# Last output projection: the first pair's parts requested ahead of the first products, in tiles of their own, and the sum weights' slabs requested one step ahead

## The chip, the cores and the metric

The kernel runs on one core of one Trainium2 chip. The metric is the device time of one execution in microseconds (us). Three runs of the kernel before gave 999.89, 1000.36 and 1002.28; the median is 1000.36 us. One more execution was taken with the hardware profiler; all views below come from that one. In them PE is TensorE's matmul, PEld its weight load, DVE is VectorE, ACT is ScalarE, POOL is GpSimd, SP is SyncE, which mostly issues DMAs; a name with a q behind it (SPq) is that engine's instruction queue.

## The reference

Two decoder layers over 1024 tokens of width 1024. What matters here is the end of each layer: three head groups give 1024 gated columns (attention 512, retention 256, gated linear attention 256), these are projected, normalised and added to the residual.

```python
a_out = sliding_window_attention(aq, ak, av, sinks) * jax.nn.silu(ag)
...
r_out = rms_norm(r).reshape(B, S, RET_W) * jax.nn.silu(rg)
...
g_out = rms_norm(g, gla_norm_gain).reshape(B, S, GLA_W) * jax.nn.silu(gg)

y = jnp.concatenate([a_out, r_out, g_out], axis=-1) @ w_out
return x + gate * rms_norm(y, post_gain)
```

All arrays are float32, and the outputs have to keep that accuracy.

## The kernel before, in words

**Numbers.** A float32 matrix is kept as two rounded halves (a high half and the rest, the low half), and a product is three passes: high by high, low by high, high by low (`PASSES`). A product of a 128-token tile's 512 input columns with a 512 x 512 block of weights is 12 matmuls of 128 x 512. Splitting is a rounding copy (high half) and a subtraction (low half); which engine does it is set in the table `EN`: "A" for ScalarE, "V" for VectorE, "G" for GpSimd.

**The last layer's projection** (`last_output`, from L1326) goes over eight token tiles t. The first two (`PLAIN = 2`) are computed one by one, the other six as three pairs. A pair of tiles (e, o), split into two column halves, and the weights, split into 2 x 2 blocks, form a 2 x 2 block product, which is done with seven block products instead of eight (Strassen's scheme in Winograd's form). It needs sums of the inputs (`Pair`) and sums of the weights (T1 to T4; W00, W10, W11 are plain blocks). The plain tiles use W00, W10, W11 and T1 too, with four products each: W00 for both tiles, then for each tile T1 and W11 into one bank and W10 into another.

**The pair's steps.** `Pair.parts` (L1280) requests four 256 KB parts from DRAM (`mixF`), one for each tile and column half. `Pair.sum` requests the plain halves of tile e (`ma<-mixS`, four DMAs) and makes four sums on VectorE (keys ms0 to ms3, L1296 to L1299). `early` splits two sums into an `mx` tile (for T2 and T1), `late` the other two (for W11 and T3). `a22` requests tile o's second half (`a<-mixS`, two DMAs) for T4. In the loop over pairs the products come in the order W00, W10, T2, T1, W11, T3, T4. After W00, `kept` (L1332) copies the bank to SBUF on ScalarE, which lets the bank go.

**The weights' sums.** `sw_second` (L593) is a job: in each of four steps k it requests four slabs of 256 KB of `w_last`, makes differences and a sum on VectorE (L569, L571, L599), and splits the three results into the arena (`sw_split`: high halves on ScalarE, L149; low halves of T2 on VectorE, of T3 and T4 on GpSimd, L564).

**Buffers.** Tags share rotating buffers: `t2` has 10 (parts, the gates' temporaries, the outputs `yg` and the residual tiles of `finish` all draw on them), `st` has 5 (weight slabs, the squares' discarded results, `a22`), `mx` has 2. PSUM banks: `mm` has 3, `aux` 5.

**The order.** TensorE runs in the order in which the program is written out. A planner keeps a clock `clk` of TensorE's estimated time and a list of jobs (generators); `pump` steps each job when its due time has come. The due times are the latencies in table `L`; `sw1` is the distance of the steps of `sw_second`. The instructions of the other engines are ordered by the framework, from the program's order and its own estimate of when operands and buffers are ready; then each engine runs its queue strictly in that order, so an instruction that waits holds up all that stand behind it. This holds for SyncE, which issues nearly all loads (`dma` with key "lw", "lmix", "lx" and so on).

**Around it.** Before the projection, the last attention jobs write their output to DRAM (`aoS<-t`), read it back transposed (`t<-aoS`), multiply it with the gate (L1581), and write it to `mixF` (unsplit) and, split (L151, L1593), to `mixS`. The pair loop's first pair is tiles 2 and 3, from the first half of the tokens; the gates that come last are of tiles 4 to 7. `finish` (L1239) reads the residual (`t<-xs`), adds, and writes the output from ScalarE's queue.

Of the kernel before, what the change touches and what calls it, by code (L numbers as in the profile page):

```python
# [10 lines left out]
F32 = mybir.dt.float32  # L11
# [6 lines left out]
P = 128  # L18
# [31 lines left out]
PLAIN = 2  # L50
# [43 lines left out]
def trunk(ctx: ExitStack, tc: tile.TileContext, ins, cst, out):  # L94
    nc = tc.nc
# [7 lines left out]
    gp = ctx.enter_context(tc.tile_pool(name="work", bufs=2))  # L103
# [9 lines left out]
    def t2(dt=F32):  # L113
        return gp.tile([P, 512], dt, tag="t2", name=nm("t2"), bufs=B2)
# [4 lines left out]
    def stage():  # L119
        return gp.tile([P, 512], F32, tag="st", name=nm("st"), bufs=BST)  # L120
# [4 lines left out]
    def mm():  # L125
        return ps.tile([P, 512], F32, tag="mm", name=nm("mm"), bufs=MMB)
# [17 lines left out]
    def eng(k):  # L144
        return G if EN[k] == "G" else V
# [37 lines left out]
    def lat(key, l):  # L183

        return L[key + "@1"] if l and key + "@1" in L else L[key]

# [257 lines left out]
    def tables_T():  # L444

        for p in range(NP_):
            yield L["tt1"]
            rep_ = t2()
# [143 lines left out]

    def sw_second():  # L593
        drain()
        for k in range(4):
            s3, x = sw_load(k, 0, 1), sw_load(k, 1, 1)
            sw_diff(s3, 1, k, x, s3)
            s2, s4 = sw_load(k, 0, 0), sw_load(k, 1, 0)
            eng("sd").tensor_tensor(s2, s3, s2, ALU.add)  # L599
# [675 lines left out]
    class Pair:  # L1275
# [10 lines left out]
        def sum(self):  # L1286
            e = self.e
            self.a = []
            for c in range(2):
                s = gp.tile([P, NT * P], F32R, tag=f"kT{c}", name=nm("ma"), bufs=1).rearrange(  # L1290
                    "p (a k q) -> p a k q", a=2, k=4)
                for a in range(2):
                    dma("lmix", f(s[:, a]), mixS[e, :, a, 4 * c:4 * c + 4])
                self.a.append(s)
            a21, a22, a11, a12 = self.p
            eng("ms0").tensor_tensor(a22, a21, a22, ALU.add)  # L1296
            eng("ms1").tensor_tensor(a21, a11, a21, ALU.subtract)
            eng("ms2").tensor_tensor(a11, a22, a11, ALU.subtract)
            eng("ms3").tensor_tensor(a12, a12, a11, ALU.subtract)  # L1299
            self.sums = a22, a11, a21, a12  # L1300
# [25 lines left out]
    def last_output(l, load_mix):  # L1326
        gcol = [modg[l][:, 0:512], modg[l][:, 512:1024]]

        def kept(src=None):
            s = gp.tile([P, 4, 129], F32, tag="smx", name=nm("kept"), bufs=SMB).rearrange("p h q -> p (h q)")[:, 0:512]  # L1330
            if src is not None:
                A.activation(s, src, AF.Copy)  # L1332
            return s
# [14 lines left out]
        nxt = None  # L1348
        if PLAIN:
            m = {0: load_mix(l, 0)}  # L1350
        for p in range(PLAIN // 2):
            x, ss, yg = [], [], []
            for t in (2 * p, 2 * p + 1):
                if t + 1 < PLAIN:
                    m[t + 1] = load_mix(l, t + 1)
                x.append(mm())
                ss.append(small(2))
                yg.append([t2(), t2()])
                prod(x[-1], slots(m[t])[0], "W00")
                if t == 0:  # L1360
                    job(sw_second())
                    pump()
            s1 = [kept(x[0]), kept(x[1])]
            for i, t in enumerate((2 * p, 2 * p + 1)):
                a = slots(m[t])
                z = aux()
                prod(z, a[0], "T1", True, False)
                prod(z, a[1], "W11", False, True)
                summed(yg[i][1], z, s1[i], ss[i][:, 1:2], 1)
                y = mm()  # L1370
                prod(y, a[1], "W10")
                summed(yg[i][0], y, s1[i], ss[i][:, 0:1], 0)
                job(finish(l, t, ss[i], yg[i]))
                if t == PLAIN - 2:
                    nxt = Pair(l, p + 1)
                    nxt.parts()
                    nxt.sum()
                pump()
                if t == PLAIN - 2:
                    nxt.early()  # L1380
                if t == PLAIN - 1:
                    nxt.late()
        for p in range(PLAIN // 2, NP_):
            cur, nxt = nxt, Pair(l, p + 1) if p + 1 < NP_ else None
            e, o = 2 * p, 2 * p + 1
# [282 lines left out]
L = {"sw1": 0.4, "ld1": 1.2, "ld2": 1.2, "ld1@1": 1.2, "ld2@1": 1.27, "swW00": 0.0, "swT1": 0.0, "swW11": 0.4, "swW10": 0.5, "tt1": 8.0, "tt2": 1.75, "tb1": 24.5, "tb2": 0.75, "pf3": 13.2, "pf1": 6.35, "pf2": 4.16, "mod1": 4.6, "mod2": 4.0, "mod3": 13.29, "mod4": 7.04, "mod5": 3.36, "mod6": 9.04, "pre1": 7.44, "kv1": 3.1, "kv2": 2.11, "aq1": 6.0, "aq7": 6.0, "ag1": 5.44, "aq2": 2.4, "aq6": 5.2, "aq3": 10.21, "aq4": 7.36, "aq5": 3.6, "hn1": 8.93, "hn2": 2.85, "gz1": 11.18, "gz2": 8.13, "gl1": 2.76, "gd3": 15.9, "gc1": 0.62, "gc2": 1.94, "gc3": 1.33, "gc4": 0.87, "gc6": 0.86, "gc5": 1.14, "rc1": 0.8, "rc2": 1.09, "rc3": 5.87, "rc4": 2.51, "fin1": 7.28, "lay1": 1.13, "gc4@1": 0.93, "mod2@1": 4.0, "mod3@1": 15.1, "mod5@1": 3.36, "mod6@1": 4.11, "pre1@1": 7.44, "kv1@1": 2.79, "kv2@1": 5.28, "aq1@1": 4.8, "aq7@1": 5.28, "ag1@1": 6.25, "aq2@1": 0.82, "aq6@1": 6.0, "aq3@1": 10.9, "aq4@1": 4.4, "aq5@1": 5.15, "hn1@1": 8.12, "hn2@1": 2.85, "gz1@1": 15.91, "gz2@1": 10.94, "gl1@1": 4.6, "gd3@1": 15.9, "gc1@1": 0.48, "gc2@1": 1.94, "gc3@1": 1.33, "gc6@1": 0.86, "gc5@1": 1.04, "rc1@1": 0.37, "rc2@1": 0.84, "rc3@1": 1.9, "rc4@1": 2.79, "fin1@1": 4.28, "lay1@1": 1.7}  # L1668
CHUNK = 7
LAG = 2  # L1670
VDB = 8
# [41 lines left out]
```

## Time and profile before

| what | value |
|---|---|
| median of three runs | 1000.36 us |
| the profiled execution's own time | 1005.29 us |
| its span, first to last instruction | 1003.6 us |
| mean granted TensorE clock | 0.989 |
| DMA moved, mean rate | 148.73 MB, 148 GB/s |

Stretches of the end of the span, by what TensorE does in them (times from the span's start; busy us of each engine, share of the DMA engines):

| stretch, us | TensorE's work | PE | DVE | ACT | DMA share |
|---|---|---|---|---|---|
| 897.0 to 906.7 | last gate projections, attention | 9.70 | 6.10 | 4.03 | 0.77 |
| 906.7 to 919.2 | W00 of tiles 0 and 1, T1 and W11 of tile 0 | 12.50 | 8.26 | 4.67 | 0.87 |
| 919.2 to 930.5 | W10 of tile 0, tile 1 | 11.30 | 7.56 | 4.81 | 0.76 |
| 944.5 to 953.0 | T1, W11, T3 of the first pair | 8.50 | 5.46 | 1.40 | 0.96 |
| 962.2 to 973.4 | second pair | 11.20 | 9.37 | 3.33 | 0.88 |
| 996.0 to 1003.6 | tail: norm, residual, store | 0.03 | 4.23 | 0.51 | 0.37 |

A view of TensorE's timeline has one line for a run of equal instructions: start, duration, engine, line of the kernel, operation, output and inputs by the program's names, shape, count, and in brackets the idle time before it with the instruction that ended it. All products have the same line, L165, a helper's.

### The profile page before, as it was taken

The page shows a single profiled execution, that of the slowest core. Times are in us where ns is not written, and L with a number is a line of the kernel's source. Part 1 is how long each engine was busy: PE and PEld are TensorE (multiplying, and loading weights), DVE is VectorE, ACT ScalarE, POOL GpSimd, SP SyncE. Part 2 cuts the span into 40 slices and gives each one's busy share as a digit, 9 for nine tenths or more (in the row PEclk, how much of TensorE's full clock was granted, in tenths as well). Part 3 has the DMA queues.
Part 4 walks back from the last instruction along what each step waited for, and adds up shares of the span by engine and source line. Part 5 has one row for each costly group of instructions (what it writes and reads, how often), then busy time and mean ns, then how long its engine had stood idle before and what let it go on. Part 6 is the DMA issues. An engine that isn't in the chain of part 4 may idle for free.

```text
span 1003.6 us, 19610 instructions
## 1 busy us (share of the span) xinstructions
PE 972.6 (97%) x7137; PEld 827.5 (82%) x7137; DVE 683.7 (68%) x1680; ACT 409.0 (41%) x1152; POOL 234.7 (23%) x275
## 2 busy tenths in 40 slices
PE   5899999999999999999999999999999999999896
PEld 1599999888998777778889999998999777777675
DVE  3788857678666778654677385775766577566786
ACT  2486312233332656632555332133333267563231
POOL 2310001223320234420122010122332034444000
PEclk8899999999999999999999999999999999999998
DMA  8842513623235355597555241352222435477883
GB/s 306 297 145 79 166 43 102 189 78 121 65 94 172 90 156 168 167 283 234 178 171 166 82 139 32 117 171 68 64 82 88 122 91 153 129 227 237 252 272 132
DMA packets 112172, 148.73 MB, mean 148 GB/s; under 512 B 11998, under 2 KB 63688, under 8 KB 112076
## 3 DMA queue, kind: packets, MB, share of 16 engines
q1 hardware_dynamic: 106380, 137.92, 44.2%
q10 hardware_dynamic: 5696, 9.56, 2.6%
q8 instruction: 56, 0.92, 0.4%
q14 instruction: 40, 0.33, 0.1%
HBM read 109.17 MB, written 36.18 MB: 145 GB/s over the span
## 4 chain that ended last, share of the span: by engine, by line
PE 80%; DMA 8%; DVE 7%; issue 2%; POOL 1%; ACT 1%; SPq 1%; ACTq 0%; POOLq 0%; DVEq 0%
PE mm L165 62%; PE aux L165 14%; PE aux L180 5%; DMA st<-in_w_in_dram 2%; DMA st<-in_w_last_dram 1%; POOL sm L635 1%; DMA xk<-in_x_dram 1%; DMA a<-mixS 1%; DMA t<-aoS 1%; DMA t<-mixF 1%; DVE arena L533 1%; DVE t L328 0%; SPq L154 0%; DMA t<-in_x_dram 0%; DMA t<-xs 0%
## 5 line engine op out<-in xcount | busy, mean ns | idle before, releaser
L165 PE MATMUL mm<-arena 128*128 128x256 f32 (+2 forms) x1824 | 300.0, 318 | 1.8 <-ACT arena L704 1.8
L165 PE MATMUL mm<-arena,arena 128*128 128x256 f32 (+2 forms) x1824 | 299.0, 317 | 0.0
L165 PEld LDWEIGHTS mm<-arena 128*128 128x128 f32 x1824 | 255.3, 191 | 26.6 <-issue 4.1
L165 PEld LDWEIGHTS mm<-arena,arena 128*128 128x128 f32 x1824 | 252.9, 188 | 25.2 <-issue 4.4
L635 POOL TENSOR_TENSOR sm<-sm,mhalf 128x1 f32<-128x1 f32 (+1 forms) x64 | 55.8, 871 | 347.0 <-DVE sm L634 328.4
L165 PE MATMUL mm<-arena,mx 128*128 128x512 f32 (+1 forms) x564 | 132.6, 392 | 3.7 <-ACT kept L1332 3.7
L165 PEld LDWEIGHTS mm<-arena,mx 128*128 128x128 f32 x564 | 103.0, 190 | 28.2 <-ACT kept L1332 4.2
L149 ACT ACTIVATE t<-aux 128x256 f32<-128x256 f32 (+2 forms) x124 | 55.7, 467 | 74.9 <-PE aux L180 63.8
L149 ACT ACTIVATE arena<-st 128x512 fp32r<-128x512 f32 x94 | 55.9, 626 | 54.8 <-DMA st<-in_w_in_dram 19.7
L533 POOL TENSOR_TENSOR arena<-st,arena 128x512 fp32r<-128x512 f32 x31 | 43.3, 1399 | 134.1 <-ACT arena L149 96.8
L923 POOL TENSOR_TENSOR smx<-smx,sm 128x512 f32<-128x512 f32 x32 | 36.5, 1142 | 127.6 <-DVE sm L922 118.4
L533 DVE TENSOR_TENSOR arena<-st,arena 128x512 fp32r<-128x512 f32 x77 | 59.5, 794 | 4.5 <-ACT arena L149 2.4
L919 ACT ACTIVATE smx<-smx,sm 128x129 f32<-128x129 f32 x128 | 49.9, 392 | 28.8 <-DVE sm L916 28.8
L180 PE MATMUL aux<-c_ident,t 128*128 128x128 f32 (+1 forms) x292 | 48.8, 284 | 5.8 <-DVE t L666 5.5
L364 DVE SCALAR_TENSOR_TENSOR acc<-st,c_act,acc 128x512 f32<-128x512 f32 x60 | 45.5, 759 | 12.6 <-DMA st<-in_w_mod_dram 12.0
L180 PEld LDWEIGHTS aux<-c_ident,t 128*128 128x128 f32 (+1 forms) x292 | 35.4, 145 | 13.5 <-DVE t L666 7.4
L698 ACT ACTIVATE t<-aux,mod,mod 128x128 f32<-128x128 f32 x68 | 26.0, 460 | 44.5 <-DVE t L1239 18.3
L165 PEld LDWEIGHTS aux<-t,mx 32*128 32x128 f32 (+1 forms) x896 | 39.5, 187 | 3.9 <-issue 1.9
L967 ACT ACTIVATE t<-aux 128x256 f32<-128x256 f32 x32 | 12.3, 384 | 73.3 <-PE aux L165 60.7
L165 PE MATMUL aux<-t,mx 32*128 32x32 f32 (+1 forms) x896 | 40.6, 272 | 0.0
L914 DVE COPY_PREDICATED smx<-c_curmask,aux 128x256 f32<-128x256 int32 x64 | 25.5, 447 | 18.9 <-ACT smx L149 15.8
L1239 DVE SCALAR_TENSOR_TENSOR t<-t,sm,t 128x512 f32<-128x512 f32 x32 | 23.9, 779 | 17.9 <-DMA t<-in_x_dram 12.3
(220 smaller groups left out, 1378.2 us busy)
## 6 DMA issues: line engine op xcount, KB each, us to landing
st<-in_w_in_dram SPq DMA_DIRECT2D x96, 256.0 KB, 3.7
st<-in_w_mod_dram SPq DMA_DIRECT2D x64, 256.0 KB, 3.0
mx<-mixS SPq DMA_DIRECT2D x20, 512.0 KB, 5.8
mixS<-t SPq DMA_DIRECT2D x72, 128.0 KB, 2.6
st<-in_w_last_dram SPq DMA_DIRECT2D x36, 256.0 KB, 3.7
wm<-in_w_mod_dram SPq DMA_DIRECT2D x12, 512.0 KB, 7.2
t<-in_x_dram SPq DMA_DIRECT2D x24, 256.0 KB, 4.3
t<-tabS SPq DMA_DIRECT2D x16, 256.0 KB, 3.7
```

The costliest lines, as they stand in the source:

```text
L149: A.activation(dst, src, AF.Copy)
L165: T.matmul(dst, lhsT, rhs, start=start, stop=stop)
L180: T.transpose(dst, src, idn)
L364: V.scalar_tensor_tensor(acc, wt, c_act[:, k:k + 1], acc, ALU.mult, ALU.add)
L533: e.tensor_tensor(lo, st, f(hi), ALU.subtract)
L635: G.tensor_tensor(r, r, mhalf[:, :w], ALU.pow)
L698: A.activation(hf[:, ks], at[kt], AF.Identity, scale=gain, bias=shift)
L914: V.copy_predicated(sv, curmask.unsqueeze(1).to_broadcast((P, 2, P)), pv[:, :, n // P - 1, :])
L919: A.activation(sm[:, h, :], sm[:, h, :], AF.Exp, bias=mx[:, h:h + 1], accum_out=sums[:, h:h + 1])
L923: eng("pn").tensor_tensor(sm[:, :, 0:128], sm[:, :, 0:128], rs.unsqueeze(2).to_broadcast((P, 4, P)), ALU.mult)
L967: A.activation(sq, po, AF.Square)
L1239: V.scalar_tensor_tensor(xt[j], yg[j], r, xt[j], ALU.mult, ALU.add)
```

## The change

It touches the last projection and two constants.

- The parts of a pair get a tag of their own, `mp`, with four buffers, instead of `t2`.
- `Pair.sum` is cut in two: `upper` requests the four `ma` tiles, `sum` makes the sums.
- For the first pair, `parts` and `upper` are called after W00 of both plain tiles, before T1 of tile 0; before, they came after W10 of tile 0. `sum` comes after tile 1's T1 and W11, `early` after its W10, and `late` after W00 of the pair and the `kept` behind it; before, `sum` and `early` came after tile 0's W10 and `late` after tile 1's. For the other pairs `upper` and `sum` stay where `sum` was.
- `sw_second` requests the slabs of step k + 1 ahead of the work of step k, and waits `sw0` after the first request. One of the four slabs of a step (`i + j == i == 1`, which is i = 1, j = 0) lies in a new tag `sx` with two buffers. The steps' distance `sw1` goes from 0.4 to 3.4 planner us; `sw0` is 2.4.
- `dynamic_dma_scratch_size=1024` is given to the program's constructor, which leaves more SBUF for tiles.

```diff
-    def sw_load(k, i, j):
-        st = stage()
+    def sw_load(k, i, j, own=False):
+        st = gp.tile([P, 512], F32, tag="sx", name=nm("sx"), bufs=2) if own else stage()
         dma("lw", st, w_last[j, 4 * i + k])
         return st
...
     def sw_second():
         drain()
+
+        def parts(k):
+            return [sw_load(k, i, j, i + j == i == 1) for i, j in ((0, 1), (1, 1), (0, 0), (1, 0))]
+
+        ahead = parts(0)
+        yield L["sw0"]
         for k in range(4):
-            s3, x = sw_load(k, 0, 1), sw_load(k, 1, 1)
+            s3, x, s2, s4 = ahead
+            if k < 3:
+                ahead = parts(k + 1)
             sw_diff(s3, 1, k, x, s3)
-            s2, s4 = sw_load(k, 0, 0), sw_load(k, 1, 0)
...
     def mpart(t, c):
-        x = t2()
+        x = gp.tile([P, 512], F32, tag="mp", name=nm("mp"), bufs=4)
...
             s1 = [kept(x[0]), kept(x[1])]
+            if p == PLAIN // 2 - 1:
+                nxt = Pair(l, p + 1)
+                nxt.parts()
+                nxt.upper()
             for i, t in enumerate((2 * p, 2 * p + 1)):
...
                 summed(yg[i][1], z, s1[i], ss[i][:, 1:2], 1)
+                if t == PLAIN - 1:
+                    nxt.sum()
                 y = mm()
                 prod(y, a[1], "W10")
                 summed(yg[i][0], y, s1[i], ss[i][:, 0:1], 0)
                 job(finish(l, t, ss[i], yg[i]))
-                if t == PLAIN - 2:
-                    nxt = Pair(l, p + 1)
-                    nxt.parts()
-                    nxt.sum()
                 pump()
-                if t == PLAIN - 2:
+                if t == PLAIN - 1:
                     nxt.early()
-                if t == PLAIN - 1:
-                    nxt.late()
...
             s1 = kept(pm)
+            if p == PLAIN // 2:
+                cur.late()
...
             a22 = cur.a22()
             if nxt:
+                nxt.upper()
                 nxt.sum()
...
-    nc = _bacc.Bacc("TRN2", target_bir_lowering=False, num_devices=1)
+    nc = _bacc.Bacc("TRN2", target_bir_lowering=False, num_devices=1, dynamic_dma_scratch_size=1024)
```

More of the change, by code (lines that the diff above doesn't have):

```diff
@@ L1284, in parts, with upper @@
             self.p = mpart(o, 0), mpart(o, 1), mpart(e, 0), mpart(e, 1)
-        def sum(self):
+            self.a = []
+        def upper(self):
             e = self.e
-            self.a = []
             for c in range(2):
@@ L1294, in sum @@
                 self.a.append(s)
+        def sum(self):
             a21, a22, a11, a12 = self.p
@@ L1667 @@
 EN = {"shw0": "V", "shw1": "A", "shw2": "A", "shw3": "A", "slw0": "V", "slw1": "G", "slw2": "V", "slw3": "G", "sht2": "A", "sht3": "A", "sht4": "A", "slt2": "V", "slt3": "G", "slt4": "G", "sd": "V", "mh0": "A", "mh1": "A", "mh2": "A", "mh3": "A", "mf": "A", "ms0": "V", "ms1": "V", "ms2": "V", "ms3": "V", "yg0": "V", "yg1": "V", "ml0": "V", "ml1": "V", "ml2": "V", "ml3": "V", "mod0": "A", "mod1": "V", "qst": "S", "smh": "S", "sml": "S", "sm0": "S", "sm1": "S", "lao": "S", "sao": "S", "lmix": "S", "ssg": "S", "lsg": "S", "ssr": "S", "lsr": "S", "lx": "S", "sx": "A", "lw": "S", "lwm": "S", "whi0": "V", "whi1": "A", "whi2": "A", "whi3": "A", "wlo0": "V", "wlo1": "V", "wlo2": "V", "wlo3": "G", "xn0": "V", "xn1": "V", "hlo0": "V", "hlo1": "V", "rot0": "V", "rot1": "V", "rdec": "V", "kslo": "V", "qslo": "V", "vlo": "G", "kT": "A", "qT": "A", "sprev": "A", "pn": "G", "pf0": "A", "aoc": "A", "hng": "V", "mh": "A", "gso": "V", "mg": "V", "mgl": "V", "rT": "A", "rv": "A", "gv": "A", "gk": "A", "ak0": "V", "ak1": "V", "ak2": "V", "ak3": "V", "kd0": "G", "kd1": "G", "kd2": "G", "kx1": "G", "kx2": "G", "kx3": "V", "kx4": "V", "qb": "G", "stx": "V"}
-L = {"sw1": 0.4, "ld1": 1.2, "ld2": 1.2, "ld1@1": 1.2, "ld2@1": 1.27, "swW00": 0.0, "swT1": 0.0, "swW11": 0.4, "swW10": 0.5, "tt1": 8.0, "tt2": 1.75, "tb1": 24.5, "tb2": 0.75, "pf3": 13.2, "pf1": 6.35, "pf2": 4.16, "mod1": 4.6, "mod2": 4.0, "mod3": 13.29, "mod4": 7.04, "mod5": 3.36, "mod6": 9.04, "pre1": 7.44, "kv1": 3.1, "kv2": 2.11, "aq1": 6.0, "aq7": 6.0, "ag1": 5.44, "aq2": 2.4, "aq6": 5.2, "aq3": 10.21, "aq4": 7.36, "aq5": 3.6, "hn1": 8.93, "hn2": 2.85, "gz1": 11.18, "gz2": 8.13, "gl1": 2.76, "gd3": 15.9, "gc1": 0.62, "gc2": 1.94, "gc3": 1.33, "gc4": 0.87, "gc6": 0.86, "gc5": 1.14, "rc1": 0.8, "rc2": 1.09, "rc3": 5.87, "rc4": 2.51, "fin1": 7.28, "lay1": 1.13, "gc4@1": 0.93, "mod2@1": 4.0, "mod3@1": 15.1, "mod5@1": 3.36, "mod6@1": 4.11, "pre1@1": 7.44, "kv1@1": 2.79, "kv2@1": 5.28, "aq1@1": 4.8, "aq7@1": 5.28, "ag1@1": 6.25, "aq2@1": 0.82, "aq6@1": 6.0, "aq3@1": 10.9, "aq4@1": 4.4, "aq5@1": 5.15, "hn1@1": 8.12, "hn2@1": 2.85, "gz1@1": 15.91, "gz2@1": 10.94, "gl1@1": 4.6, "gd3@1": 15.9, "gc1@1": 0.48, "gc2@1": 1.94, "gc3@1": 1.33, "gc6@1": 0.86, "gc5@1": 1.04, "rc1@1": 0.37, "rc2@1": 0.84, "rc3@1": 1.9, "rc4@1": 2.79, "fin1@1": 4.28, "lay1@1": 1.7}
@@ new lines @@
+L = {"sw0": 2.4, "sw1": 3.4, "ld1": 1.2, "ld2": 1.2, "ld1@1": 1.2, "ld2@1": 1.27, "swW00": 0.0, "swT1": 0.0, "swW11": 0.4, "swW10": 0.5, "tt1": 8.0, "tt2": 1.75, "tb1": 24.5, "tb2": 0.75, "pf3": 13.2, "pf1": 6.35, "pf2": 4.16, "mod1": 4.6, "mod2": 4.0, "mod3": 13.29, "mod4": 7.04, "mod5": 3.36, "mod6": 9.04, "pre1": 7.44, "kv1": 3.1, "kv2": 2.11, "aq1": 6.0, "aq7": 6.0, "ag1": 5.44, "aq2": 2.4, "aq6": 5.2, "aq3": 10.21, "aq4": 7.36, "aq5": 3.6, "hn1": 8.93, "hn2": 2.85, "gz1": 11.18, "gz2": 8.13, "gl1": 2.76, "gd3": 15.9, "gc1": 0.62, "gc2": 1.94, "gc3": 1.33, "gc4": 0.87, "gc6": 0.86, "gc5": 1.14, "rc1": 0.8, "rc2": 1.09, "rc3": 5.87, "rc4": 2.51, "fin1": 7.28, "lay1": 1.13, "gc4@1": 0.93, "mod2@1": 4.0, "mod3@1": 15.1, "mod5@1": 3.36, "mod6@1": 4.11, "pre1@1": 7.44, "kv1@1": 2.79, "kv2@1": 5.28, "aq1@1": 4.8, "aq7@1": 5.28, "ag1@1": 6.25, "aq2@1": 0.82, "aq6@1": 6.0, "aq3@1": 10.9, "aq4@1": 4.4, "aq5@1": 5.15, "hn1@1": 8.12, "hn2@1": 2.85, "gz1@1": 15.91, "gz2@1": 10.94, "gl1@1": 4.6, "gd3@1": 15.9, "gc1@1": 0.48, "gc2@1": 1.94, "gc3@1": 1.33, "gc6@1": 0.86, "gc5@1": 1.04, "rc1@1": 0.37, "rc2@1": 0.84, "rc3@1": 1.9, "rc4@1": 2.79, "fin1@1": 4.28, "lay1@1": 1.7}
```

## The prediction

> **What bounds the kernel now.** I read the page's busy shares first, then the chain of waits over the last 170 us, then TensorE's and SyncE's own timelines there, because the diff touches nothing before layer 1's output projection.
>
> ```profile
> PE 972.6 (97%) x7137; PEld 827.5 (82%) x7137; DVE 683.7 (68%) x1680; ACT 409.0 (41%) x1152; POOL 234.7 (23%) x275
> ```
>
> TensorE is busy 97% of the span, so an edit can give back only what TensorE still waits or runs slowly in the stretch that it touches. TensorE's timeline of that stretch (start, duration, what, idle before it and the releaser):
>
> ```profile
> 906.72 5.86 PE L165 MATMUL mm<-arena,mx 128*128 128x512 f32 x24
> ...
> 919.25 2.97 PE L165 MATMUL mm<-arena,mx 128*128 128x512 f32 x12
> ...
> 927.68 2.98 PE L165 MATMUL mm<-arena,mx 128*128 128x512 f32 x12
> 930.49 5.79 PE L165 MATMUL mm<-arena,ma 128*128 128x512 f32 x24
> 939.99 4.61 PE L165 MATMUL mm<-arena,mx 128*128 128x512 f32 x12 [3.72 <-ACT kept L1332]
> 944.45 2.97 PE L165 MATMUL aux<-arena,mx 128*128 128x512 f32 x12
> 947.26 5.77 PE L165 MATMUL mm<-arena,mx 128*128 128x512 f32 x24
> 953.78 2.99 PE L165 MATMUL mm<-arena,a 128*128 128x512 f32 x12 [0.75 <-DMA a<-mixS]
> ```
>
> Twelve matmuls are one product. 906.72 is W00 of tiles 0 and 1; 919.25 and 927.68 are W10 of tiles 0 and 1; 930.49 is W00 and W10 of the first pair; 939.99 is T2, 944.45 T1, 947.26 W11 and T3, 953.78 T4. Two waits stand there: 3.72 us before T2 and 0.75 us before T4. T2 itself takes 4.61 us where its neighbours take 2.97. The view by stretch (length, busy times, granted clock, DMA share, GB/s) says why:
>
> ```profile
> 906.70:919.20 12.50, 12.50 (x59) 9.55 (x58) 8.26 (x12) 4.67 (x9) 5.32 (x5) 1.00 0.87 264
> ...
> 936.20:940.00 3.80, 0.08 (x2) 0.01 (x1) 3.80 (x9) 2.47 (x5) 0.00 (x0) 1.00 0.44 159
> 940.00:944.50 4.50, 4.50 (x13) 3.55 (x14) 3.54 (x8) 0.72 (x2) 0.57 (x1) 0.62 0.75 216
> 953.00:962.20 9.20, 8.45 (x37) 6.88 (x37) 7.91 (x15) 3.33 (x8) 0.93 (x1) 1.00 0.81 260
> 981.80:996.00 14.20, 14.20 (x73) 11.83 (x71) 8.48 (x17) 2.72 (x9) 0.79 (x2) 1.00 0.31 111
> ```
>
> Behind the idle 3.72 us the granted clock is 0.62, and it is 1.00 again afterwards; behind the idle 0.75 us it stays 1.00. So the hole costs 3.72 + (4.61 - 2.97) = 5.36 us, the T4 wait 0.75 us, together 6.11 us. Nothing else is to be had: the last row shows TensorE busy without a break to 996.0.
>
> Why is T2 late? Its bank is let go by `kept` (L1332), though W00, which `kept` copies, ended near 933.4 (half of the row at 930.49). ScalarE's timeline shows what stood ahead of `kept`, and VectorE's the sums:
>
> ```profile
> 933.55 0.63 ACT L149 ACTIVATE mx<-t 128x512 fp32r<-128x512 f32 x1 [2.61 <-PE mm L165]
> 935.55 0.63 ACT L149 ACTIVATE mx<-t 128x512 fp32r<-128x512 f32 x1 [1.36 <-DVE t L1298]
> 937.86 0.63 ACT L149 ACTIVATE mx<-t 128x512 fp32r<-128x512 f32 x1 [0.37 <-DVE t L1239]
> 939.36 0.58 ACT L1332 ACTIVATE kept<-mm 128x512 f32<-128x512 f32 x1
> ...
> 932.78 0.69 DVE L1296 TENSOR_TENSOR t<-t,t 128x512 f32<-128x512 f32 x1 [0.44 <-DMA t<-mixF]
> 934.83 0.68 DVE L1298 TENSOR_TENSOR t<-t,t 128x512 f32<-128x512 f32 x1
> 937.36 0.68 DVE L1270 TENSOR_TENSOR mx<-t,mx 128x512 fp32r<-128x512 f32 x1
> ```
>
> All four splits of the pair's sums (a fourth lies between) are queued on ScalarE ahead of `kept`, and they wait for the sums, and these for the parts. The chain of waits, with SyncE's queue, gives the root:
>
> ```profile
> 922.12 0.28 ACT t L149
> ...
> 922.42 2.48 DMA aoS<-t
> ...
> 926.48 6.20 DMA t<-mixF
> ...
> 879.27 0.38 SPq L154 DMA_DIRECT2D mixF<-t  x1
> ...
> 925.93 1.88 SPq L154 DMA_DIRECT2D t<-mixF  x4
> ```
>
> The parts were written at 879.27, but requested only at 925.93, behind the last attention output's round trip through DRAM. They land at 932.69.
>
> **The change, part by part.** *Parts and upper halves requested ahead.* The same eight requests (four parts, four `ma`, 256 KB each) go out, from a place in the program one T1+W11+W10 earlier: from the end of tile 0's W10 (919.25 + 2.97 = 922.2) to the end of tile 1's W00 (906.72 + 5.86 = 912.6), 9.6 us of TensorE. No byte and no instruction is added. The parts no longer take four of the ten `t2` buffers. What must happen for T2 to start on time, at 936.2: the second sum's low half (937.36 + 0.68 = 938.04 now) is needed four matmuls into T2, at 937.2. So parts landing 1 us earlier suffice for it, and 2 us do with margin. If SyncE moves the request as far, it goes out at 916.3 and lands, after the same 6.76 us (925.93 to 932.69), at 923.1: eight us more than needed. Gain from 0 (nothing lands earlier) to 5.36; I take it whole together with the next part.
>
> *`late` behind the copy.* The two splits at 936.86 and 937.86 are now emitted after `kept`. With sums ready and only two splits ahead, `kept` ends at worst at 933.4 + 2 x 0.63 + 0.58 = 935.2, and the bank is free in time. W11 needs the third split at 936.2 + 2 x 2.81 = 941.8 (2.81 is the step from 927.68 to 930.49); 935.2 + 0.63 + 0.68 is 936.5. Nothing added: 0; without that cover (VectorE was busy for all of 936.2 to 940.0), it is bounded by 0.7 us, one queued VectorE operation.
>
> *The sums later in the program*, behind the add of tile 1's first output (T1+W11 ends about 927.7): four sums of 0.69 end at 931.2 at the earliest, then split 0.63 and low half 0.68: 932.5. Cover 3.7 us; at worst the sums do not start before 932.78 as now, which is the zero end of the first part.
>
> *Slabs one step ahead.* The sixteen slabs stay sixteen. Steps are spaced 3.4 instead of 0.4 planner us, the last one 2.4 + 3 x 3.4 = 12.6 after W00 of tile 0 (909.6). A product costs 12 x 512 / 2400 = 2.56 planner us and 2.81 measured, so that is 909.6 + 13.8 = 923.4.
>
> ```profile
> 915.79 1.03 DVE L569 SCALAR_TENSOR_TENSOR st<-st,gnc,st 128x512 f32<-128x512 f32 x1 [0.57 <-DMA st<-in_w_last_dram]
> 918.14 1.27 DVE L599 TENSOR_TENSOR st<-st,st 128x512 f32<-128x512 f32 x1 [1.31 <-DMA st<-in_w_last_dram]
> 923.31 0.73 DVE L599 TENSOR_TENSOR st<-st,st 128x512 f32<-128x512 f32 x1 [1.19 <-DMA st<-in_w_last_dram]
> 927.14 1.29 POOL L564 TENSOR_TENSOR arena<-st,arena 128x512 fp32r<-128x512 f32 x1 [1.95 <-ACT arena L149]
> ```
>
> With the slabs there, four VectorE operations of about 0.7, three splits of 0.63 and two POOL operations of 1.29 follow: 923.4 + 2.8 + 2.6 = 928.8 (one POOL operation covers two splits), against 928.4 now and T2 at 936.2. Price 0, slack 7 us. The VectorE waits on slabs (0.57 + 1.31 + 1.19 here) are what it may fill with sums and adds; off the path, so counted at 0. As ScalarE's last attention copy (922.12) was queued among these splits, it can come earlier too.
>
> *Own tiles and a smaller DMA scratch.* The page lists these queues:
>
> ```profile
> q1 hardware_dynamic: 106380, 137.92, 44.2%
> q10 hardware_dynamic: 5696, 9.56, 2.6%
> q8 instruction: 56, 0.92, 0.4%
> q14 instruction: 40, 0.33, 0.1%
> ```
>
> Every transfer that the program asks for is on SyncE's or ScalarE's queue, none on POOL's. Price 0. [...]
>
> *T4 of the first pair, what is late next.* TensorE reaches it at 953.78 - 0.75 - 5.36 = 947.67. Its `a` tiles stand behind the next pair's parts in SyncE's queue:
>
> ```profile
> SPq L154 <- DVE t L151: 6.2, 2, 5.5
> ...
> 942.27 1.88 SPq L154 DMA_DIRECT2D t<-mixF  x4
> ...
> 945.22 4.38 SPq L154 DMA_DIRECT2D a<-mixS  x2
> ...
> 945.22 8.43 DMA a<-mixS
> ```
>
> SyncE stood 5.5 us at once for the last gate's rounding copy (L151), which VectorE reached at 938.56 behind the sums and splits. If that wait goes, `a` lands at 953.64 - 5.5 = 948.14, and T4 waits about 0.5 us instead of 0.75. If none of it goes, T4 waits 953.78 - 947.67 = 6.11 and the next product runs slowly for 1.64 more: +7.00 on this term. Bounds -0.75 and +7.00; I take 0, near the lower end, because that row names an operation which the early sums free.
>
> **The sum.** The profiled execution took 1005.29 us, 1.69 beyond its span of 1003.6, and 4.93 more than the median of 1000.36. Minus 5.36 gives 999.93 for it; I take the same difference off the median: 1000.36 - 5.36 = **995.0**.
>
> **Rivals.** *(B) T4 takes the wait over.* The own tiles for parts are four, and the next pair's parts need the buffers that `late` frees; if the last low half still ends near 942, as the requests at 942.27 suggest, `a` stays at 953.64. Then 1000.36 - 5.36 + 7.00 = 1002.0. For it: SyncE serves its requests in the order shown, parts before `a`. Against it: the 5.5 us wait ahead of them. Where the wait moves by half it stays under what slowed the clock, and the result is near 998.
>
> *(C) The change does not do what it says.* DMA share is 0.87 at 264 GB/s while the parts should now come, so they may land where they did, and the hole stays: 1000.4. Against it: one us earlier is enough.
>
> *(D) Slower: SyncE's head of line.* Slabs one step ahead want six stage buffers plus one or two own ones; stage buffers are five. The sixth request stands at SyncE's head until a step's splits are done, with parts and `ma` behind it.
>
> ```profile
> 909.61 2.37 SPq L154 DMA_DIRECT2D st<-in_w_last_dram  x4
> ...
> 914.65 5.14 SPq L154 DMA_DIRECT2D st<-in_w_last_dram  x4
> ```
>
> Four requests took 5.14 there against 2.37. If three steps cost 5.14 each ahead of the eight pair requests (0.47 each), the last part is asked for at 909.61 + 2.37 + 3 x 5.14 + 8 x 0.47 = 931.2 and lands 6.2 later, at 937.4, 4.7 after 932.69: 1000.36 + 4.7 = 1005.1. It decides from a last request later than 926.5. Against it: the parts come before steps two to four in the program, and need no stage buffer.
>
> [...]
>
> **How the numbers follow.** Forecast 0.58, B 0.17, C 0.10, D 0.15. About 0.3%, 3.0 us, is what a measurement tells from no change: faster is below 997.4, slower above 1003.4. The forecast is faster throughout (993.8, both waits and 0.5 of scatter, to 997.3), B is the same except for its half-moved edge (0.02 faster), C the same, D slower: 0.60, 0.25, 0.15. The range runs from 993.5 to B's 1002.0 and leaves out D and little else; the forecast's own is 993.8 to 997.3.
>
> **What would show it.** Right: parts requested before 920, no idle before T2, T2 near 2.97 at clock 1.00, `kept` ahead of two of the splits, T4's wait under 2 us. B: T4 idle above 3 us. C: T2's hole as before. D: SyncE waiting on stage buffers, parts after 926. A new hole before 930 would make all of it wrong.

## The result, and the profile after

The changed kernel took 1003.9 us (median of 9 runs, 1002.9 to 1006.82), the kernel before, run beside it, 1000.78 us (9 runs, 998.01 to 1003.93). The ratio is 1.0033 (95%: 1.0016 to 1.0049): slower by about 3.3 us (all gains and losses below are the ratio less one, of some 1000 us), where 5.4 us of gain were forecast. The profiled execution of the changed kernel took 1003.9 us, its span is 1002.2 us.

The busy shares on the page of the changed kernel hardly differ:

```profile
PE 971.0 (97%) x7137; PEld 826.4 (82%) x7137; DVE 687.1 (69%) x1680; ACT 408.3 (41%) x1152; POOL 240.3 (24%) x275
```

TensorE's timeline of the changed kernel (start, duration, what, idle before it and the releaser):

```profile
894.79 0.65 PE L165 MATMUL aux<-t,va 128*64 128x256 f32 x4
897.31 0.65 PE L165 MATMUL aux<-t,vd 128*64 128x256 f32 x4 [1.87 <-POOL t L941]
...
909.50 5.86 PE L165 MATMUL mm<-arena,mx 128*128 128x512 f32 x24
...
939.42 3.01 PE L165 MATMUL mm<-arena,mx 128*128 128x512 f32 x12 [0.36 <-ACT arena L149]
...
950.64 2.91 PE L165 MATMUL mm<-arena,a 128*128 128x512 f32 x12
...
960.75 3.00 PE L165 MATMUL mm<-arena,mx 128*128 128x512 f32 x12 [1.50 <-DVE t L1345]
```

T2 of the first pair (939.42) waits 0.36 us and runs in 3.01, T4 (950.64) waits not at all: the waits that the change was to remove are gone there. The second pair's T2 (960.75) waits 1.50 us. And at 897.31, in the last attention heads and ahead of the whole projection, there is a wait of 1.87 us that was not there before. GpSimd's, VectorE's and SyncE's timelines of the changed kernel, in this order, show where it comes from:

```profile
894.82 1.39 POOL L930 TENSOR_TENSOR smx<-smx,sm 128x512 f32<-128x512 f32 x1 [3.92 <-DVE sm L929]
896.17 2.12 POOL L941 TENSOR_SCALAR_AFFINE_SELECT t<-t 128x512 f32<-128x512 f32 x2
```

```profile
893.02 0.69 DVE L1305 TENSOR_TENSOR mp<-mp,mp 128x512 f32<-128x512 f32 x1 [2.09 <-DMA mp<-mixF]
893.89 0.69 DVE L1306 TENSOR_TENSOR mp<-mp,mp 128x512 f32<-128x512 f32 x1 [0.18 <-DMA mp<-mixF]
894.50 0.17 DVE L929 RECIPROCAL sm<-sm 128x4 f32<-128x4 f32 x1
```

```profile
883.22 0.38 SPq L154 DMA_DIRECT2D mp<-mixF  x1
...
886.49 2.61 SPq L154 DMA_DIRECT2D mp<-mixF  x3
...
890.96 7.19 SPq L154 DMA_DIRECT2D st<-in_w_last_dram  x3
898.72 0.38 SPq L154 DMA_DIRECT2D t<-aoS  x1
...
923.90 0.93 SPq L154 DMA_DIRECT2D t<-aoS  x2
```

The parts are requested at 883 to 889, not near 916. Two of the sums made of them (L1305, L1306) stand in VectorE's queue ahead of the reciprocal that ends an attention softmax (L929). VectorE idles 2.09 us for the parts, and the reciprocal is done only at 894.7. GpSimd has idled 3.92 us for it when it normalises (L930), then it masks (L941), and TensorE waits for that. Behind the parts, three slab requests stretch over 7.19 us of SyncE's queue. Most of that is no issuing: SyncE waits for stage buffers, 3.8 us of it for an earlier slab to land (its view of waits, 888 to 899). Attention's next read back (`t<-aoS`) goes out at 898.72.

The same places in another execution of the kernel before (label before_b below), in VectorE's, SyncE's and TensorE's timeline, in this order:

```profile
888.82 0.18 DVE L922 RECIPROCAL sm<-sm 128x4 f32<-128x4 f32 x1
891.15 0.69 DVE L571 TENSOR_TENSOR st<-st,st 128x512 f32<-128x512 f32 x1 [2.15 <-DMA st<-in_w_last_dram]
```

```profile
887.86 0.33 SPq L154 DMA_DIRECT2D st<-in_w_last_dram  x1
...
888.72 4.14 SPq L154 DMA_DIRECT2D st<-in_w_last_dram  x3
...
893.44 0.38 SPq L154 DMA_DIRECT2D t<-aoS  x1
...
920.18 0.92 SPq L154 DMA_DIRECT2D t<-aoS  x2
921.19 1.88 SPq L154 DMA_DIRECT2D t<-mixF  x4
```

```profile
892.59 0.65 PE L165 MATMUL aux<-t,va 128*64 128x256 f32 x4
893.08 0.60 PE L165 MATMUL aux<-t,vd 128*64 128x256 f32 x4
...
905.22 5.86 PE L165 MATMUL mm<-arena,mx 128*128 128x512 f32 x24
...
934.73 3.03 PE L165 MATMUL mm<-arena,mx 128*128 128x512 f32 x12
...
946.61 3.32 PE L165 MATMUL mm<-arena,a 128*128 128x512 f32 x12 [0.41 <-DMA a<-mixS]
```

There no sum stands ahead of the reciprocal. It comes 3.77 us ahead of the product `aux<-t,va` (892.59), against 0.29 in the changed kernel (894.79), and `aux<-t,vd` follows without a wait. The three slab requests stretch over 4.14 us, and the read goes out 0.85 us behind that product, against 3.93.

Executions already differ by some us before this stretch, so single profiles are best compared by stretches of TensorE's timeline: A from the attention product `aux<-t,va` at 892 to 896 (894.79 above) to W00 of the plain tiles (909.50), B from there to W00 of the first pair (`mm<-arena,ma`), C from there to the end of the last matmul. Each is a difference of two starts in TensorE's timeline, the last of a start and an end:

| profile | A, us | B, us | C, us | sum |
|---|---|---|---|---|
| before, the prediction's | 12.63 | 23.77 | 65.54 | 101.94 |
| before_a | 12.62 | 23.78 | 61.59 | 97.99 |
| before_b | 12.63 | 23.77 | 61.44 | 97.84 |
| before_c | 12.62 | 23.78 | 61.64 | 98.04 |
| before_d | 12.63 | 23.77 | 61.07 | 97.47 |
| after | 14.71 | 23.78 | 61.37 | 99.86 |
| after_a | 17.27 | 23.78 | 59.54 | 100.59 |
| x_sw | 12.62 | 23.78 | 58.96 | 95.36 |
| x_sw_tight | 12.62 | 24.18 | 60.55 | 97.35 |
| x_pair | 18.36 | 23.78 | 61.40 | 103.54 |
| x_mp | 17.26 | 23.77 | 59.25 | 100.28 |
| x_t2 | 12.62 | 23.78 | 64.35 | 100.75 |
| x_copy | 12.62 | 23.78 | 64.34 | 100.74 |
| e1_first_sums | 12.63 | 25.51 | 63.49 | 101.63 |
| e2_all_sums | 12.62 | 25.25 | 63.16 | 101.03 |
| x_mp_hold | 12.62 | 27.50 | 63.19 | 103.31 |
| after_hold | 12.62 | 27.87 | 60.32 | 100.81 |

The table already says most: the execution on which the prediction rests is alone among five with 65.5 us in C; the changed kernel loses 2.1 and 4.6 us in A; and no profile has less than 58.96 us in C. A shorter C behind a longer A (after_a, x_mp) is no gain: their sums are above those of before_a to before_d.

### The profile page after: what moved, and what is told of

It is laid out like the page before. It is cut to its first block, busy times and chain, and to the rows that moved or that the text cites. A ratio compares the mean times of both kernels' runs of the same rounds, so it can differ in the third digit from the quotient of the medians.

```text
span 1002.2 us, 19595 instructions
## 1 busy us (share of the span) xinstructions
PE 971.0 (97%) x7137; PEld 826.4 (82%) x7137; DVE 687.1 (69%) x1680; ACT 408.3 (41%) x1152; POOL 240.3 (24%) x275
## 4 chain that ended last, share of the span: by engine, by line
PE 80%; DVE 8%; DMA 5%; issue 3%; POOL 2%; ACT 1%; ACTq 0%; POOLq 0%; SPq 0%; DVEq 0%
PE mm L165 62%; PE aux L165 14%; PE aux L180 5%; DMA st<-in_w_in_dram 2%; DMA xk<-in_x_dram 1%; POOL sm L642 1%; POOL arena L564 1%; DVE t L1246 1%; DVE arena L533 1%; DMA sx<-in_w_last_dram 1%; DMA mp<-mixF 0%; DVE t L328 0%; DMA aoS<-t 0%; DVE mx L1277 0%; DVE t L1345 0%
## 5 line engine op out<-in xcount | busy, mean ns | idle before, releaser
L149 ACT ACTIVATE arena<-st 128x512 fp32r<-128x512 f32 x90 | 53.5, 625 | 49.4 <-PE mm L165 18.3
L930 POOL TENSOR_TENSOR smx<-smx,sm 128x512 f32<-128x512 f32 x32 | 37.1, 1158 | 128.9 <-DVE sm L929 121.8
```

What stands on the lines that cost most here:

```text
L149: A.activation(dst, src, AF.Copy)
L930: eng("pn").tensor_tensor(sm[:, :, 0:128], sm[:, :, 0:128], rs.unsqueeze(2).to_broadcast((P, 4, P)), ALU.mult)
```

## The experiments

Ratios are to runs of the kernel before on the same chip, with 95% intervals; waits are read from each kernel's profile. Numbers of lines shift where an edit adds lines.

**The kernel before again.** No edit.

> The kernel before, unedited, profiled again. Theory 1 (the hole ahead of T2 is not in every execution): its one profiled execution was 1005.29 us against a median of 1000.8 us, 4.5 above, so a second profile shows an own time near 1000.8 us and a T2 wait of at most 2 us, with T2 near 3.0 us at clock 1.00. Rival (the hole is always there and the changed kernel loses elsewhere): the wait is 3 to 4 us again, T2 takes 4 us or more, and the own time is near 1005.

> The kernel before, unedited, a third profile. Theory 1: T2's wait varies from execution to execution, and the own time varies with it, by the wait and the slow clock together (up to 5.4 us). Rival: the same wait in all of them, and the own time varies for other reasons.

> The kernel before again. Theory 1: no wait above 1 us ahead of the first pair's T2, own time 998 to 1002. Rival: the hole of 3 to 4 us, own time near 1005.

> The kernel before again, as the one above: theory 1 has no wait above 1 us ahead of the first pair's T2; the rival has the hole of 3 to 4 us.

> The changed kernel, unedited, profiled again, for the scatter between executions: a wait of TensorE behind POOL near 897 of 1.5 to 3.5 us in this one too, with a slow clock behind it where it is above 2.5 us, and no wait of over 1 us ahead of the first pair's T2. Rival: the wait near 897 belonged to one execution and is under 1 us here.

The four took 1001.65, 999.68, 1002.93 and 999.54 us. In the timeline of before_b above, T2 of the first pair (934.73) does not wait and runs in 3.03 us. Across the four it waited about 0.1, 0, 1.41 and 0.68 us, always with 3.02 or 3.03 us for T2 itself; T4 waited 1.20, 0.41, 0.51 and 1.05. before_c, with 1.41 us and 1002.93, lies outside what was expected of it (no wait above 1 us, 998 to 1002), but it has no hole either. The 5.36 us hole of the prediction is in one of five executions. The second profile of the changed kernel (1002.53 us) has the wait in stretch A again, 2.86 us, with a granted clock of 0.76 from 896 to 903.

**The sums held back, not the requests.** In the changed kernel the first pair's sums (`e1_first_sums`), then all pairs' sums (`e2_all_sums`), are put behind the add of the last output made before them in VectorE's queue:

```diff
-            V.tensor_tensor(dst, bank, s, ALU.add)
+            added[0] = V.tensor_tensor(dst, bank, s, ALU.add)
...
-                    nxt.sum()
+                    with tc.issue_after(added[0].ins):
+                        nxt.sum()
```

> The changed kernel with the first pair's four sums held, in VectorE's queue, behind the add of tile 1's first output, their place in the program. Theory 2 (the sums, queued by the framework 40 us ahead of their place, stand in VectorE's queue waiting for the parts, and attention's reciprocal behind them is late): the 1.87 us wait of TensorE near 897 goes, and the time falls by 1.5 to 2.2 us against the changed kernel's 1003.9, to about 1002. Rival (DMA traffic of the early parts delays attention): the wait near 897 stays at 1.5 us or more and the time stays near 1003.9.

> The same for the sums of all pairs: each behind the add that precedes it in the program. Theory 2: the 1.50 us wait ahead of the second pair's T2 goes as well (the sums of the third pair no longer stand ahead of that product's bank release), and the time falls to 1000.0 to 1001.0 us, the kernel before's. Rival (that wait comes from VectorE's load or from SyncE's waits for the four part buffers): it stays above 1 us, and the time equals the kernel with only the first pair held.

Measured: 1005.89 us, ratio 1.0056 (1.0036 to 1.0075), and 1006.32 us, 1.0063 (1.0039 to 1.0088). The wait at 897 goes, and so does the 1.50 us wait before the second pair's T2, but the time does not come back: about 1002 and 1000.0 to 1001.0 were expected. TensorE's timeline of e1_first_sums:

```profile
911.59 0.65 PE L165 MATMUL aux<-t,va 128*64 128x256 f32 x4 [0.89 <-ACT t L149]
912.80 0.65 PE L165 MATMUL aux<-t,vd 128*64 128x256 f32 x4 [0.56 <-POOL t L941]
...
937.61 1.20 PE L165 MATMUL mm<-arena,mx 128*128 128x512 f32 x4 [1.46 <-ACT kept L1341]
939.96 2.11 PE L165 MATMUL mm<-arena,mx 128*128 128x512 f32 x8 [1.16 <-DVE mx L1277]
```

Attention now waits 15 us later (0.89 + 0.56), and T2 waits 1.46 + 1.16 for `kept` and for the low half, since the sums are late. e2_all_sums shows the same waits in the same places (0.61 + 0.56 and 0.77 + 1.15).

**The change's two parts apart.** `x_sw` is the kernel before with the slabs alone requested one step ahead (with `sx`, `sw0`, the wide `sw1` and the smaller scratch). `x_pair` is the changed kernel with just that undone. The edit in both is the one of `sw_second` in the change:

```diff
+        ahead = parts(0)
+        yield L["sw0"]
         for k in range(4):
-            s3, x = sw_load(k, 0, 1), sw_load(k, 1, 1)
+            s3, x, s2, s4 = ahead
+            if k < 3:
+                ahead = parts(k + 1)
```

`x_mp` is the kernel before with only the own tiles for parts and the smaller scratch. `x_t2` is the changed kernel with the parts back in the shared buffers. For `x_mp` the edit is this, for `x_t2` its reverse:

```diff
     def mpart(t, c):
-        x = t2()
+        x = gp.tile([P, 512], F32, tag="mp", name=nm("mp"), bufs=4)
```

> The kernel before with the slabs alone changed: requested one step ahead, one of four in its own tile, steps 3.4 planner us apart, and the smaller scratch. Theory 3 (what the change costs is the parts' own tiles, which let the first pair's sums go in VectorE's queue ahead of two of attention's reciprocals): in this kernel the sums stand behind all reciprocals, no wait near 897, time within 1.5 us of before (999 to 1002.5). Rival 3a (the wider steps put VectorE work of the weight sums beside the first pair and make T2 or the second pair wait): a wait of 1 us or more ahead of T2, time 1002 or more.

> The changed kernel with the slabs' part undone (as before: no slab ahead, steps 0.4). Theory 3: the sums stand ahead of two reciprocals as in the changed kernel, so the wait of about 1.9 us near 897 is there and the time is the changed kernel's, 1003 to 1004.5. Rival 3a: most of the loss is gone, 1000 to 1002.

> The kernel before with nothing but the parts' own four tiles (and the smaller scratch); the places in the program stay. Theory 3: it is the tiles, not the place in the program, that lets the requests and sums float ahead: the sums again stand ahead of two reciprocals, wait of 1.5 to 2.5 us near 897, time 1002.5 to 1004.5. Rival 3b (the place in the program decides): no wait there, time as before, 999 to 1002.

> The changed kernel with the parts back in the shared buffers, all else of the change kept. Theory 3: the requests have to wait for a shared buffer, the sums stand behind all reciprocals, the wait near 897 is gone (0 to 0.5 us), and the time is 1000 to 1002. Rival 3a: no gain against the changed kernel, 1003 or more.

| kernel | us, runs | ratio (95%) |
|---|---|---|
| x_sw | 998.58, 12 | 0.9976 (0.9963 to 0.999) |
| x_pair | 1005.62, 6 | 1.0055 (1.0033 to 1.0076) |
| x_mp | 1003.3, 12 | 1.0036 (1.002 to 1.0051) |
| x_t2 | 1004.07, 12 | 1.0035 (1.0018 to 1.0053) |

The slabs' part alone gains 2.4 us, and `x_sw` is the fastest kernel here; it and `x_pair` lie just outside the times expected of them (999 to 1002.5, 1003 to 1004.5). The own tiles alone cost 3.6 us. The smaller scratch, which goes with them in `x_mp`, is not the cause: `x_sw` and `x_sw_tight` (below) have it too and lose nothing. TensorE's and SyncE's timelines of x_mp, and the view by stretch of its 6.6 us behind the wait (length, busy us of TensorE, of its weight loads, of VectorE, ScalarE and GpSimd, granted clock, DMA share, GB/s):

```profile
896.47 0.65 PE L165 MATMUL aux<-t,vd 128*64 128x256 f32 x4 [2.85 <-POOL t L934]
```

```profile
881.99 0.38 SPq L154 DMA_DIRECT2D mp<-mixF  x1
```

```profile
896.40:903.00 6.60, 6.53 (x26) 4.84 (x26) 5.28 (x10) 2.52 (x10) 2.14 (x4) 0.74 0.86 238
```

One changed tag gives the same wait at the same place: 2.85 us, with the granted clock at 0.74 behind it; with W00 at 910.23 and the product before the wait at 892.97, A is 17.26. The program asks for the parts where it always did, behind the plain tile's W10. So it was the shared buffer that kept the framework from issuing the request and the sums far ahead (the first part goes out at 881.99 in x_mp, the four at 921.19 in before_b, some 40 us later).

`x_t2` was a miss. The parts wait for a buffer again and stretch A is clean, but VectorE's, TensorE's and SyncE's timelines show a new loss:

```profile
917.95 0.69 DVE L1305 TENSOR_TENSOR t<-t,t 128x512 f32<-128x512 f32 x1 [4.68 <-DMA t<-mixF]
```

```profile
940.54 4.58 PE L165 MATMUL mm<-arena,mx 128*128 128x512 f32 x12 [3.67 <-ACT arena L149]
```

```profile
911.91 1.81 SPq L154 DMA_DIRECT2D t<-mixF  x4
...
929.07 0.86 SPq L154 DMA_DIRECT2D st<-in_w_last_dram  x2
```

Now the parts go out at 911.91, VectorE stands 4.68 us at the first sum with the weights' sums queued behind it, the last slabs are requested at 929.07, and T2 waits 3.67 us for a split of the weights (`arena`, ScalarE). The first sum holds up what stands behind it in VectorE's queue for these 4.68 us, as late sums held up T2 in e1 (1.46 + 1.16 us).

**Why the slabs' part gains.** `x_sw_tight` is `x_sw` with the old distance of the steps:

```diff
-L = {"sw0": 2.4, "sw1": 3.4, ...
+L = {"sw0": 0.4, "sw1": 0.4, ...
```

> The kernel before with the slabs requested one step ahead and the own tile, but the steps 0.4 planner us apart as before. Theory 5 (the gain of the slabs' part, 998.6 against 1000.4, comes from the wider steps, which let attention's last output copy and its round trip go ahead of the weight sums' splits): most of the gain is gone, 999.6 to 1001.5, and the read back of attention's last output is issued about 15 us after W00's start as before (12 with the wide steps). Rival 5a (it comes from the request one step ahead): 998 to 999.2.

Measured 1000.3 us (12 runs), 1.0001 (0.9992 to 1.001): no gain. So the request ahead does not help by itself, and the distance of the steps is needed for the gain; wide steps without the request ahead were not tried. Timelines of x_sw, TensorE's and then SyncE's:

```profile
904.99 5.86 PE L165 MATMUL mm<-arena,mx 128*128 128x512 f32 x24
...
934.39 2.91 PE L165 MATMUL mm<-arena,mx 128*128 128x512 f32 x12
...
945.51 2.91 PE L165 MATMUL mm<-arena,a 128*128 128x512 f32 x12
```

```profile
916.64 0.93 SPq L154 DMA_DIRECT2D t<-aoS  x2
917.67 1.88 SPq L154 DMA_DIRECT2D t<-mixF  x4
```

No wait is left at T2 and T4. Attention's last read back goes out 916.64 - 904.99 = 11.65 us after W00; in before_b it is 920.18 - 905.22 = 14.96, in x_sw_tight 924.82 - 908.81 = 16.01. With wide steps the last weights' work no longer stands ahead of the round trip, on which parts, gates and `a` hang. That the gain comes from there is argued from these profiles and was not tried by itself, and in the profile of the changed kernel the earlier round trip is not seen: there it is 923.90 - 909.50 = 14.40.

The same distance tells the prediction's execution apart. SyncE's timeline of it has the read back here:

```profile
924.92 0.92 SPq L154 DMA_DIRECT2D t<-aoS  x2
```

That is 924.92 - 906.72 = 18.20 us after W00, with 65.54 us in C; in before_a to before_d it is 14.96 to 16.22, with 61.07 to 61.64. So the hole goes with a late round trip, and a late round trip is not in every execution.

**Is it the order of the sums, or the early megabyte?** The first sum alone is held behind attention's last reciprocal, in `x_mp` (`x_mp_hold`) and in the changed kernel (`after_hold`):

```diff
-        V.reciprocal(rs, sums)
+        recip[0] = V.reciprocal(rs, sums)
...
-            eng("ms0").tensor_tensor(a22, a21, a22, ALU.add)
+            with tc.issue_after(recip[0].ins):
+                eng("ms0").tensor_tensor(a22, a21, a22, ALU.add)
```

> The kernel before with the parts' own tiles alone, and the first of the sums held in VectorE's queue behind the last reciprocal of attention. Theory 4 (own tiles cost time only through that order in the queue): the wait of 2.85 us near 896 and the slow clock behind it go, time 999.0 to 1001.5, against 1003.3 with the tiles alone. Rival 4a (the early megabyte of parts delays the slabs and attention's round trips): a wait of over 1 us stays before W00, time 1002 or more.

> The changed kernel with the same hold: the first pair's sums behind the last reciprocal of attention, no further back. Theory 4: the wait of 1.87 us near 897 goes and nothing takes its place, time 1000.0 to 1002.3. Rival 4b (as when the sums were held far back, the third and fourth step of the weight sums are late, and T2 waits for them): a wait of 1.5 us or more ahead of T2, time 1003 to 1006.

Measured 1005.11 us, 1.0046 (1.0033 to 1.006), and 1005.0 us, 1.0051 (1.0032 to 1.0069). So the sums' place is not the whole cost: stretch A is clean in both, and B takes 3.7 and 4.1 us more instead. VectorE's and TensorE's timelines of x_mp_hold:

```profile
895.07 0.69 DVE L572 TENSOR_TENSOR st<-st,st 128x512 f32<-128x512 f32 x1 [5.42 <-DMA st<-in_w_last_dram]
```

```profile
913.12 0.65 PE L166 MATMUL aux<-t,va 128*64 128x256 f32 x4 [1.39 <-ACT t L149]
914.29 0.83 PE L166 MATMUL aux<-t,vd 128*64 128x256 f32 x4 [0.52 <-POOL t L935]
915.05 7.23 PE L166 MATMUL aux<-arena,mx 128*128 128x512 f32 x24
```

VectorE waits 5.42 us for a slab (2.15 in before_b), and the next attention heads come late. So the traffic was tried by itself: `x_copy` is the kernel before (with the smaller scratch), its sums in the old order, and the first pair's parts requested a second time, early, into own tiles that nobody reads.

```diff
+            if self.e == PLAIN:
+                for t, c in ((o, 0), (o, 1), (e, 0), (e, 1)):
+                    x = gp.tile([P, 512], F32, tag="mp", name=nm("mp"), bufs=4)
+                    dma("lmix", x.rearrange("p (k q) -> p k q", k=4), mixF[t, :, 4 * c:4 * c + 4, :])
```

> The kernel before, with the first pair's four parts requested a second time, into own tiles that nothing reads; the requests stand at the same place in SyncE's queue as with the own tiles alone, and the sums read the shared buffers in the old order. Theory 6 (the early megabyte itself is the cost: it pushes back slabs and attention's round trips at a stretch where the DMA engines are busy): 1002 to 1005, with TensorE waits of 1 us or more between 890 and 941. Rival 6a (the cost is in the queues' order of sums and slabs): 999.5 to 1001.5, no such wait.

Measured 1004.44 us (11 runs), 1.0028 (1.0017 to 1.004). SyncE's and VectorE's timelines of x_copy, a row of its chain of waits (a slab's way from request to landing), and its view by stretch (columns as above):

```profile
881.68 0.90 SPq L154 DMA_DIRECT2D mp<-mixF  x1
...
889.46 6.33 SPq L154 DMA_DIRECT2D st<-in_w_last_dram  x3
896.36 0.38 SPq L154 DMA_DIRECT2D t<-aoS  x1
...
924.05 0.92 SPq L154 DMA_DIRECT2D t<-aoS  x2
```

```profile
893.70 0.69 DVE L571 TENSOR_TENSOR st<-st,st 128x512 f32<-128x512 f32 x1 [4.01 <-DMA st<-in_w_last_dram]
```

```profile
888.56 5.12 DMA st<-in_w_last_dram
```

```profile
876.00:890.00 14.00, 14.00 (x86) 10.00 (x85) 10.38 (x24) 10.24 (x38) 6.32 (x8) 1.00 0.90 275
```

One more megabyte in this place costs 2.8 us although nobody waits for it. The slab requested at 888.56 needs 5.12 us to land; in before_b the one requested at 887.86 has landed by 891.15, 3.29 us later. The three slab requests behind the parts stretch over 6.33 us of SyncE's queue (4.14 in before_b), where the single one at 888.56 takes 0.33 us to issue, VectorE waits 4.01 us for a slab (2.15), and the read back goes out 896.36 - 893.29 = 3.07 us behind stretch A's start (0.85). In before_b the same 14 us had a DMA share of 0.80 at 236 GB/s; here it is 0.90 at 275.

Stretch A is clean in x_copy all the same; its loss lies in C, 64.34 us, with a wait of 2.94 us before T2. The last read back goes out 924.05 - 905.91 = 18.14 us after W00, as late as in the prediction's execution (18.20), which has such a hole without the copy. So this one profile does not prove the path from the copy to the hole; the ratio over 11 runs shows its cost. And x_copy keeps the later request of the same parts, which the kernels with own tiles do not have, so its 2.8 us is not a measured share of their cost.

## Why the prediction was wrong

**The sum: its one term was mis-sized.** It subtracted 5.36 us from the median of the runs, a hole read from an execution that had itself taken 4.93 us more than this median. That excess is the hole for the most part: C is 65.54 us there and 61.07 to 61.64 in the four others, so the hole belongs to that execution and not to the median. What can be had in C is 61.4 - 59.0 = 2.4 us by the table, and 2.4 us is what `x_sw` gains. With the mechanism left as it was, the sum would have been near 998, not 995.0.

**"If SyncE moves the request as far, it goes out at 916.3": this step failed.** The request moved by about 40 us, to 883, since the own tiles never wait for a buffer. `x_mp` shows that the tiles alone do it, without a move of the calls. "Own tiles ... price 0" looked at bytes and queues and not at what the shared `t2` buffers had done, which was to hold the request back. In its place stand about 3.6 us of cost (2.0 to 5.1, `x_mp`). In the profiles of x_mp and of the changed kernel they show as the wait in stretch A, which the prediction did not look at: sums queued ahead of attention's reciprocals, and waiting for their parts. But taking that order away gives nothing back (`x_mp_hold`, `after_hold`, e1, e2), and an early megabyte costs 2.8 us even where no sum depends on it (`x_copy`), ahead of slabs for which VectorE waits even without it (2.15 us in before_b). How the 3.6 us split between the two, and why the hold makes it no better, stays open beyond the waits shown.

**"The sums later in the program": wrong in the same way.** They came earlier in VectorE's queue than before, not later. Their place in the program, which x_mp does not even change, did not bind their place in VectorE's queue.

**Slabs one step ahead, price 0: wrong in the other direction.** The prediction noted that the last attention copy could come earlier and set it at nothing. The slabs' part is the one gain in the change: 2.4 us alone, and the difference between `x_pair` (+5.5 us) and the changed kernel (+3.3 us) is of the same size, though these two intervals overlap and the earlier round trip that goes with the gain in `x_sw` is not in the changed kernel's profile.

**`late` behind `kept`: the time held, the order did not.** T2 waits 0.36 us in the profile after, but not because `kept` overtook the splits. ScalarE's timeline:

```profile
935.47 1.14 ACT L149 ACTIVATE mx<-mp 128x512 fp32r<-128x512 f32 x2
...
938.71 0.63 ACT L149 ACTIVATE arena<-sx 128x512 fp32r<-128x512 f32 x1 [2.10 <-DVE sx L569]
939.24 0.58 ACT L1341 ACTIVATE kept<-mm 128x512 f32<-128x512 f32 x1
```

The last two splits of the pair's sums still stand ahead of `kept`, which ends at 939.82. The prediction allowed 935.2 at worst, 938.0 here, since W00 (909.50) is 2.78 us later than in its profile. T2 starts at 939.42, so it did not wait for that copy; what ended its wait was the weights' split at 938.71. So the "slack 7 us" of the slabs' part did not hold either: this split ends at 939.34, where 928.8 was reckoned, 931.6 here. That T2 could start without the copy was not foreseen, and why it did not wait for it here, as in the kernel before, stays open.

**T4 at 0: held, and for the reason given.** The last gates' rounding copies (L151 on VectorE) start at 934.01 and 935.75 in the profile after, against 938.56 and 939.70, and T4 waits nothing.

**Rivals.** None was right. B did not come: the parts and `a` were in time. C did not come: the hole is gone, but it was there in one of five executions only. D forecast 1005.1, which is near the time measured by luck: it came from stage buffers and late parts, and the parts came too early, not too late. D reckoned with SyncE's queue in its own stretch alone and did not ask what was queued where the request would really land. There a slab behind the early parts took 5.12 us from request to landing (x_copy), where one took at most 3.29 in before_b and one requested at 889.36 took 4.48 in the prediction's execution, both without early parts. How much of it the parts add, and how, these single profiles do not show. The prediction's last sentence named the sign that came true, a new hole before 930, without a chance for it.

## What to carry to other kernels

Before a wait of one profile is put into a sum, ask whether that execution stands above the median by about the same amount; if so, the wait may be scatter and not a gain to be had, and more profiles of the same kernel tell. A buffer that a load shares with other work is also what keeps the load from going out early: give it its own tile only after finding out where in each engine's queue the load and its consumers will then stand, and how busy the DMA engines are there (a share of 0.80 in before_b and 0.90 in x_copy, from 876 to 890). When requests are spaced, look at what gets ahead of them; here the gain of wider steps went with a round trip that no longer stood behind them.

## What was not expected of the hardware

A granted clock well below 1.00 followed waits shorter than the 3.72 us that the prediction had seen: after 2.67 us idle (x_pair) the clock was 0.50 for the next 6.6 us, after 2.85 us (x_mp) it was 0.74 over the same length, and after 1.39 + 0.52 us with one short product between them (x_mp_hold, rows above) it was 0.78 from 914.0 to 921.6, and the product of 24 matmuls took 7.23 us instead of the 5.89 it takes in before_b. After 1.87 us (after) it did not follow: 1.00 from 897.3 to 903. Nor does the length of the waits alone decide: after 0.77 + 1.15 us with four matmuls between (e2_all_sums) the clock was 0.72 from 938 to 944 and the next eight matmuls took 3.67 us, after 1.46 + 1.16 us with four between (e1_first_sums) the same eight took 2.11. What decides it, these runs do not show. But a wait of 2.85 us can cost more than its length: A grew by 4.64 us in x_mp for a wait of 2.85.

Executions of one kernel also differ ahead of all touched work: the start of stretch A lies between 892.59 and 895.52 in the five profiles of the kernel before, nearly as far apart as in all seventeen (892.22 to 896.19).
